# A diagonal complex recurrence over token chunks as rotated real scans, with its parameter tables moved one stage ahead

## Chip, core and metric

One core of a Trainium2 chip runs the whole kernel. The metric is the device time of one execution in microseconds (us), lower is better. PE is the matrix engine, PEld its weight loads, DVE the vector engine, ACT the scalar engine, POOL the general engine, SP the engine whose queue issues nearly all DMAs.

## The reference, cut to what matters

The program is one inference step of a two-layer network on 512 latent and 128 context tokens of 1024 channels. Each layer normalizes, projects, runs three mixers side by side (a Hyena long convolution, an S5 state space mixer, a gated DeltaNet), gates and projects their outputs, adds them up and projects again. The change concerns the S5 mixer: 64 groups of 16 channels, each with a diagonal state of 64 complex numbers, scanned forward and backward.

```python
for d in range(2):                               # forward, backward
    lam = lax.complex(lam_re[d], lam_im[d])
    step = jnp.exp(log_step[d])[:, None]
    lam_bar = jnp.exp(lam * step)                # parameters only
    b_bar = ((lam_bar - 1.0) / lam)[..., None] * lax.complex(b_re[d], b_im[d])
    seq = ug if d == 0 else jnp.flip(ug, axis=1)
    bu = jnp.einsum('gph,blgh->blgp', b_bar, seq.astype(jnp.complex64))
    bu = bu.at[:, 0].add(lam_bar * init)
    _, xs = lax.associative_scan(_lin_combine, (broadcast(lam_bar), bu), axis=1)
    finals.append(xs[:, -1])
    yd = einsum(c_re, xs.real) - einsum(c_im, xs.imag)
    y = y + (yd if d == 0 else jnp.flip(yd, axis=1))
```

`lam_bar` does not depend on the data: its powers, `b_bar` and the read-out factors are functions of the parameters alone.

## The kernel before, in words

The residual stream is kept transposed, channels on partitions and the 640 tokens along the free axis. Every projection (`load_w`, `mm3`, `proj`) splits weights and activations into a high and a low part and runs three float32r products; ACT writes the high part of the weights (L69), DVE or POOL the low part (L70), PE multiplies (L91). PE tile names tell who asks: `pj` is a projection of a mixer or of the merge, `pg` is one of 40 gate column tiles or the Hyena branch projection. The `pg` work depends only on the normalized input, so it can stand anywhere after it.

`start` loads the tokens, transposes them and computes the first modulation vectors. Then each layer has three stages. The first runs S5 and Hyena in turns, eight column tiles of 128 channels each: `run` takes one step of `s5_core`, then one of `hyena`, and so on, and emits 14 of the gate tiles behind them (L190). The second is the DeltaNet (`gdn`) with the other gate tiles. The third is `merge`: GLU of the S5 output, branch projections, output projection, residual, sums of squares for the next norm. `norm_h` stands at the head of a layer.

The code does not write out the order on an engine. A planner takes the instructions, walks a simulated time and gives each engine, whenever it is free there, the ready instruction that was emitted first. On the chip each engine, and each DMA queue, then keeps that order: an instruction that waits holds all that stands behind it on its engine. The layer-1 tables of the kernel before stand in the trace well ahead of their layer for that reason.

In S5, `s5_tables` (L685) makes the powers 0 to 8 of `lam_bar` (`PR`, `PI`), its powers over 8, 16, .. 128 tokens (`LR`, `LI`, `L2`) and the factor of `b_bar`, at the head of `s5_core`. The tokens lie in chunks of 8, 80 chunks in all (64 latent, 16 context). For each column tile:

- `s5_in` (L773) projects the input, sends it through DRAM (`us`) into the layout `U` (8 tokens x 16 channels on partitions, groups and chunks along the free axis), forms the increment matrices `M2` on DVE and POOL (L824 to L829), transposes them on PE, copies them out (L835), multiplies by `U` (L839, with 96 columns) and copies the state increments of the 80 chunks to `X`, laid out chunk, re/im, group (L841, ACT). Forward states lie on partitions 0 to 63, backward ones on 64 to 127.
- `s5_scan` (L845) runs the recurrence. Five segments of 16 chunks go side by side, and 16 steps follow one another. Each step is five DVE instructions on at most 80 elements, which write `Z` and `W` (`step`, L884 to L888), and two ACT copies that put the state before the step into `X` in place of the increment (L895). Then the states that enter the later segments are carried over (`C`) and their contributions added to `X` (`D`, `E`, L912 to L916). POOL makes the powers of the chunk step for that (`FR`, `FI`, L865 to L871).
- `s5_out` (L919) forms read-out matrices `M3` (L949 to L954), the kernels of the convolution inside a chunk (`K`, through DRAM `ks`, to `M1`), and sums three products per group: two of `M3` with `X`, whose columns lie 16 elements apart (L981, L982), and one of `M1` with `U` (L983).

`s5_in` and `s5_scan` of tile i + 1 are emitted ahead of `s5_out` of tile i. The S5 part has one PSUM bank (`pms`).

Of the kernel before, what the change touches and what calls it, by code (L numbers as in the profile page):

```python
# [20 lines left out]
NLAT = 512  # L21
# [17 lines left out]
# column tiles (128 wide) of the packed weights  # L39
# [13 lines left out]
def bc(ap, shape):  # L53
    return ap.to_broadcast(shape)


class Net:
# [4 lines left out]
    # ---------------------------------------------------------------- helpers  # L62
# [24 lines left out]
    def mm3(self, o, kh, wh, wl, xh, xl, s, m=128):  # L87
        """o += w^T x[:, s] over k tiles 4 kh .. 4 kh + 3"""
# [13 lines left out]
    def proj(self, l, t, xh, xl, q):  # L102
        """column tile t of x @ w: [128, 640] on two banks"""
# [8 lines left out]
    def conv(self, y, P, w, b, t=None):  # L112
        """3 taps along the tokens of each segment; t: space that moves a tap to ACT and Pool"""
# [26 lines left out]
    def wrap(self, pool, x, shape, phase, tag):  # L140
        """x (+ pi/2 if phase) folded into [-pi, pi]"""
# [13 lines left out]
    # ---------------------------------------------------------------- whole  # L155
# [75 lines left out]
    def start(self):  # L231
        """x^T with the grid embedding, sums of squares, first modulation vectors"""
        tc, nc, a = self.tc, self.nc, self.a
        self.xd = [self.dp.tile([KT, 128, NTOK], F32, name="xd%d" % i) for i in range(self.depth)]
# [17 lines left out]
        with self.pool(name="st", bufs=2) as p:  # L252
            xi = [p.tile([128, DM], F32, name="xi%d" % t, bufs=1) for t in range(5)]
            for t in range(5):
                nc.sync.dma_start(xi[t], a["x"][t * 128:(t + 1) * 128])
            pos = [p.tile([128, KT // 2, NLAT], F32, name="pos%d" % h, bufs=1) for h in range(2)]
            for h in range(2):
                nc.sync.dma_start(pos[h], a["pos"][4 * h:4 * h + 4].rearrange("k p t -> p k t"))
            wm = []
            for s in range(4):  # L260
                wm.append(p.tile([128, KT, 4, 128], F32, name="wm%d" % s, bufs=1))
# [1402 lines left out]
```

## Time and profile before

| | |
|---|---|
| time, median of 3 runs | 3792.77 us (3789.83 to 3797.14) |
| span of the profiled execution | 3792.6 us |
| PE busy | 3401.0 us (90%) |
| DVE busy | 2607.9 us (69%) |
| POOL busy | 1692.8 us (45%) |
| ACT busy | 1521.2 us (40%) |
| mean granted clock of PE | 0.941 |
| DMA | 362.89 MB, 96 GB/s, 16 engines 32% busy |

The stages of the profiled execution, in us from its start: start and first norm to 55, S5 and Hyena of layer 0 to about 1003, DeltaNet to about 1660 and merge, overlapping, to about 1940, norm to 1963, S5 and Hyena of layer 1 to about 2910, DeltaNet to about 3500, merge and final norm to the end.

[...]

### The profile page before, as it was taken

Reading aid. Unit: us, or ns where it says so; the run is one execution under the profiler, and the core shown is the slowest. Engines: PE = TensorE matmul, PEld = TensorE weight load, DVE = VectorE, ACT = ScalarE, POOL = GpSimd, SP = SyncE. Lnnn points to the kernel's source line nnn. Section 1 sums busy time; section 2 is a strip of 40 time slices with the busy share of each in tenths; the row PEclk is TensorE's granted clock in tenths of the full one; section 3 lists DMA queues with packets and bytes.
Section 4 is the critical chain, followed back from the end, with each engine's and each line's share of the span. In section 5 each row is a group of like instructions: output and inputs, shape, how many; then the busy total and the mean of one; then the engine's idle time right before and its main releaser. Section 6 shows DMA issues by size and latency. Waiting matters only on the chain. (4 is left out here: it accounts for less than half of the span.)

```text
span 3792.6 us, 70255 instructions
## 1 busy us (share of the span) xinstructions
PE 3401.0 (90%) x25850; PEld 3246.1 (86%) x25850; DVE 2607.9 (69%) x6113; ACT 1521.2 (40%) x3519; POOL 1692.8 (45%) x2083
## 2 busy tenths in 40 slices
PE   6898988888989898899978899899899898798998
PEld 5788977788989888899977889898889898798998
DVE  6988788889237874643749788878883278776354
ACT  4533333333244555443334333333332445555422
POOL 4656555555344444301226565666654454351010
PEclk8899999999989999899989999999999899899999
DMA  6322233432231212543632222222222312224352
GB/s 226 113 75 67 75 94 103 119 97 58 79 86 63 71 60 71 175 141 111 197 104 77 73 65 73 75 81 72 72 61 73 96 63 78 61 92 140 126 176 89
DMA packets 310615, 362.89 MB, mean 96 GB/s; under 512 B 86814, under 2 KB 190270, under 8 KB 310016
## 3 DMA queue, kind: packets, MB, share of 16 engines
q1 hardware_dynamic: 305368, 357.75, 31.0%
q8 instruction: 204, 3.34, 0.4%
q10 hardware_dynamic: 4904, 0.66, 0.1%
q14 instruction: 139, 1.14, 0.1%
HBM read 291.74 MB, written 66.54 MB: 94 GB/s over the span
## 5 line engine op out<-in xcount | busy, mean ns | idle before, releaser
L91 PE MATMUL pj<-hh,wh 128*128 128x320 f32 x2048 | 670.7, 328 | 77.5 <-ACT wh L69 32.4
L91 PE MATMUL pj<-hl,wh 128*128 128x320 f32 x2048 | 662.0, 323 | 2.4 <-DVE hl L70 2.4
L91 PE MATMUL pj<-hh,wl 128*128 128x320 f32 x2048 | 660.0, 324 | 2.8 <-POOL wl L70 1.5
L69 ACT CAST wh<-wr 128x512 fp32r<-128x512 f32 x608 | 375.0, 618 | 598.4 <-PE pj L91 396.9
L70 POOL TENSOR_TENSOR wl<-wr,wh 128x512 fp32r<-128x512 f32 x288 | 382.4, 1331 | 517.0 <-ACT wh L69 466.9
L91 PEld LDWEIGHTS pj<-hh,wh 128*128 128x128 f32 x2048 | 404.3, 197 | 89.7 <-ACT wh L69 33.7
L91 PE MATMUL pg<-hh,wh 128*128 128x320 f32 x1280 | 416.6, 326 | 14.1 <-ACT wh L69 10.2
L91 PE MATMUL pg<-hl,wh 128*128 128x320 f32 x1280 | 412.8, 323 | 0.0
L70 DVE TENSOR_TENSOR wl<-wr,wh 128x512 fp32r<-128x512 f32 x320 | 244.1, 764 | 244.5 <-ACT wh L69 242.1
L91 PE MATMUL pg<-hh,wl 128*128 128x320 f32 x1280 | 409.9, 324 | 1.6 <-POOL wl L70 1.6
L91 PEld LDWEIGHTS pj<-hl,wh 128*128 128x128 f32 x2048 | 403.2, 197 | 6.5 <-DVE hl L70 5.3
L91 PEld LDWEIGHTS pj<-hh,wl 128*128 128x128 f32 x2048 | 402.4, 197 | 5.9 <-POOL wl L70 2.8
L91 PE MATMUL pj<-yh,wh 128*128 128x320 f32 x1024 | 316.8, 311 | 3.6 <-ACT yh L69 2.4
L91 PE MATMUL pj<-yl,wh 128*128 128x320 f32 x1024 | 317.4, 311 | 2.4 <-DVE yl L70 2.3
L91 PE MATMUL pj<-yh,wl 128*128 128x320 f32 x1024 | 316.4, 310 | 0.0
L895 ACT COPY X<-Z 64x80 f32<-64x80 f32 x512 | 131.1, 256 | 386.7 <-DVE Z L888 380.1
L91 PEld LDWEIGHTS pg<-hh,wh 128*128 128x128 f32 x1280 | 252.1, 197 | 18.9 <-ACT wh L69 11.3
L91 PEld LDWEIGHTS pg<-hh,wl 128*128 128x128 f32 x1280 | 249.1, 196 | 4.1 <-POOL wl L70 2.7
L91 PEld LDWEIGHTS pg<-hl,wh 128*128 128x128 f32 x1280 | 251.7, 197 | 0.7 <-issue 0.4
L888 DVE TENSOR_TENSOR Z<-Z,X 64x80 f32<-64x80 f32 x512 | 209.0, 408 | 13.7 <-ACT X L841 1.1
L91 PEld LDWEIGHTS pj<-yh,wh 128*128 128x128 f32 x1024 | 192.5, 189 | 4.9 <-ACT yh L69 3.2
L91 PEld LDWEIGHTS pj<-yl,wh 128*128 128x128 f32 x1024 | 192.8, 188 | 4.2 <-DVE yl L70 4.2
(513 smaller groups left out, 8757.1 us busy)
## 6 DMA issues: line engine op xcount, KB each, us to landing
wr<-in_wt SPq DMA_DIRECT2D x608, 256.0 KB, 2.7
gt<-gst SPq DMA_DIRECT2D x160, 160.0 KB, 2.0
gt<-gt SPq DMA_DIRECT2D x64, 320.0 KB, 3.3
wr<-in_wmod SPq DMA_DIRECT2D x64, 256.0 KB, 3.1
Pm<-gcd SPq DMA_DIRECT2D x32, 320.0 KB, 11.2
wm<-in_wmod SPq DMA_DIRECT2D x4, 2048.0 KB, 18.6
M<-ks SPq DMA_DIRECT2D x256, 32.0 KB, 1.8
xd<-x SPq DMA_DIRECT2D x16, 320.0 KB, 4.3
```

Of the source, the lines that this page charges most:

```text
L69: self.nc.scalar.copy(h, src)
L70: (eng or self.nc.vector).tensor_tensor(l, src, h.bitcast(F32), op=ALU.subtract)
L91: ins = self.nc.tensor.matmul(o, w[:, k, :m], x[:, kh * 4 + k, s], start=kh == 0 and k == 0 and i == 0, stop=kh == 1 and k == 3 and i == 2)
L888: nc.vector.tensor_tensor(out[h], out[h], x, op=ALU.add)
L895: nc.scalar.copy(xv, S[h])
```

## The change

The complex factor over a chunk is split into its modulus and a turn. Increments are turned back by the power of the turn that belongs to their chunk, then the recurrence has a real factor and needs one real scan for the real part and one for the imaginary part, along all chunks of all eight groups at once; the result is turned forward again. The columns of a group are now 83: a slot for the initial state, 64 latent chunks, a slot, 16 context chunks, a slot. The factor array `A` holds the modulus in the chunk columns and 0 in the slots, where the state is reset.

- `s5_scan` is gone, with its 16 steps, the carries and the POOL powers. In `s5_in` the PSUM result is not copied by ACT; four DVE instructions per 3, 3 and 2 groups turn it into `X`. Then four scan instructions (re and im, forward partitions and backward partitions) write `Z`. A new `s5_turn` turns `Z` into the states with six DVE instructions of 664 elements.
- `X` is now re/im, group, chunk, so that a group's columns are contiguous for the read-out products.
- The turns `E` (2 x 8 x 83 per tile) and a block `F` (8 x 73: powers for `M2` and `M3`, initial states, modulus, `b_bar`) depend on parameters alone. `s5_tables` computes them and writes them to DRAM, 664 KB and 292 KB per column tile; `s5_in` loads both back. For layer 0 this is emitted in `start`, ahead of the loads of `x`, position table and modulation weights, with the turns doubled on DVE, two tiles at a time; for layer 1 in `merge` of layer 0, between the branch projections and the output projection, with the turns doubled on POOL, one tile at a time. `b_bar`, made per tile by POOL in `s5_in` before, and the powers that ACT copied per tile (`T2`, `T3`), are in `F` now.
- The small loads go out on SP (parameters) and ACT (`sbr`, `sbi`). In `merge` the gate tile `gt` has 3 buffers instead of 4.

The diff, cut to its core (comments that it deletes and unchanged parts left out):

```diff
@@ start
+            tab = self.s5_tables(0, nc.vector, 2)
+            next(tab)
             for t in range(5):
                 nc.sync.dma_start(xi[t], a["x"][t * 128:(t + 1) * 128])
+            next(tab)
             for h in range(2):
                 nc.sync.dma_start(pos[h], ...)
             for s in range(4):
                 nc.sync.dma_start(wm[s], ...)
+            for _ in tab:
+                pass
@@ s5_tables
+        with self.pool(name="s5k", bufs=1) as cp:
+            with self.pool(name="s5t", bufs=1) as p:
+                T = self.s5_factors(l, cp, p)
+            yield 0
+            with self.pool(name="s5u", bufs=1) as p:
+                for c0 in range(0, 8, n):
+                    self.s5_turns(l, c0, n, p, T, eng)
+        yield 1
@@ s5_turns (new), H = 8 n groups
+        E = p.tile([128, 2, H, 83], F32, name="tE", bufs=nc_)
+        eng.tensor_copy(E[:, :, :, 1], T["V"][:, :, gq])
+        e = 1
+        while e < 82:
+            n = min(e, 82 - e)
+            s, d = slice(1, 1 + n), slice(e + 1, e + 1 + n)
+            sh = [128, 2, H, n]
+            t = x[:, :, :, 0:n]
+            eng.tensor_tensor(t, E[:, :, :, s], bc(E[:, 1:2, :, e:e + 1], sh), op=ALU.mult)
+            eng.tensor_tensor(E[:, :, :, d], E[:, :, :, s], bc(E[:, 0:1, :, e:e + 1], sh), op=ALU.mult)
+            eng.tensor_tensor(E[:, 0, :, d], E[:, 0, :, d], t[:, 1], op=ALU.subtract)
+            eng.tensor_tensor(E[:, 1, :, d], E[:, 1, :, d], t[:, 0], op=ALU.add)
+            e *= 2
...
+            nc.sync.dma_start(te[c0 + c].rearrange(...), E[:, :, s])
+            nc.sync.dma_start(tf[c0 + c].rearrange(...), F[:, s])
@@ s5_core
         for i in range(8):
-            now = st
+            now = self.s5_turn(l, i, p)
             if i < 7:
                 self.s5_in(l, i + 1, p, T)
-                st = self.s5_scan(l, i + 1, p, T)
             self.s5_out(l, i, p, T, *now)
@@ s5_in
+        F = p.tile([128, H, 73], F32, name="F5", bufs=2)
+        nc.sync.dma_start(F, T["tf"][ct].rearrange("p (g c) -> p g c", g=H))
...
+        E = p.tile([128, 2, H, 83], F32, name="E5")
+        nc.sync.dma_start(E, T["te"][ct].rearrange("p (r g c) -> p r g c", r=2, g=H))
+        for x, n in ((slice(1, 65), 64), (slice(66, 82), 16)):
+            nc.scalar.copy(A[:, :, x], bc(F[:, :, 40:41], [128, H, n]))
...
-        for st in range(2):
+        for g1, k in ((0, 3), (3, 3), (6, 2)):
...
-                    nc.tensor.matmul(pi[:, g * 128:g * 128 + 96], mt[:, g, :], U[:, gi * 80:gi * 80 + 96], ...)
-                nc.scalar.copy(X[:, :, r, ls].rearrange("p j g -> p g j"), ...)
+                    nc.tensor.matmul(pi[:, r, g, :], mt[r][:, g, :], U[:, g1 + g, :], start=True, stop=True)
+            x = X[:, :, ls, 1:83]
+            nc.vector.tensor_tensor(x, pi, bc(E[:, 0:1, ls, 1:83], sh), op=ALU.mult)
+            nc.vector.tensor_tensor(w, pi, bc(E[:, 1:2, ls, 1:83], sh), op=ALU.mult)
+            nc.vector.tensor_tensor(x[:, 0], x[:, 0], w[:, 1], op=ALU.add)
+            nc.vector.tensor_tensor(x[:, 1], x[:, 1], w[:, 0], op=ALU.subtract)
...
+        for r in range(2):
+            z, b = [y[:, r].rearrange("p g c -> p (g c)") for y in (Z, X)]
+            nc.vector.tensor_tensor_scan(z[lo], A[lo], b[lo], 0.0, op0=ALU.mult, op1=ALU.add)
+            nc.vector.tensor_tensor_scan(z[hi, n - 3::-1], A[hi, n - 1:1:-1], b[hi, n - 1:1:-1], 0.0, ...)
@@ s5_turn (new)
+        for r in range(2):
+            nc.vector.tensor_tensor(X[:, r], Z[:, r], re, op=ALU.mult)
+            nc.vector.tensor_tensor(W, Z[:, 1 - r], im, op=ALU.mult)
+            nc.vector.tensor_tensor(X[:, r], X[:, r], W, op=ALU.add if r else ALU.subtract)
@@ s5_out
-                nc.tensor.matmul(o, M3[:, 0, g, 1:9, :], X[:, :, 0, gi], start=True, stop=False)
+                nc.tensor.matmul(o, M3[:, 0, g, 1:9, :], X[:, 0, gi, 0:82], start=True, stop=False)
@@ merge
+        if l + 1 < self.depth:
+            for _ in self.s5_tables(l + 1, nc.gpsimd, 1):
+                pass
```

## Rows read from the trace of the kernel before

**Rows 1.** Busy time of the engines, the page.
```profile
PE 3401.0 (90%) x25850; PEld 3246.1 (86%) x25850; DVE 2607.9 (69%) x6113; ACT 1521.2 (40%) x3519; POOL 1692.8 (45%) x2083
```
**Rows 2.** Stretches: length; busy PE, PEld, DVE, ACT, POOL; PE clock, DMA share, GB/s.
```profile
0.00:55.00 55.00, 25.21 (x315) 19.14 (x315) 22.73 (x74) 14.88 (x33) 7.38 (x7) 0.81 0.88 317
50.00:200.00 150.00, 124.47 (x764) 115.52 (x765) 135.77 (x312) 79.87 (x185) 112.16 (x130) 0.85 0.34 107
200.00:1000.00 800.00, 715.00 (x5603) 664.52 (x5602) 652.58 (x1547) 274.51 (x747) 450.75 (x626) 0.95 0.30 85
2000.00:2100.00 100.00, 79.54 (x556) 74.31 (x555) 95.85 (x225) 46.89 (x132) 61.26 (x86) 0.91 0.25 74
2100.00:2900.00 800.00, 737.94 (x5404) 706.68 (x5404) 634.99 (x1461) 281.43 (x752) 466.76 (x628) 0.95 0.26 72
900.00:1000.00 100.00, 94.01 (x697) 88.85 (x697) 61.28 (x126) 24.11 (x58) 46.92 (x50) 0.98 0.30 73
2800.00:2900.00 100.00, 93.45 (x690) 89.32 (x690) 66.49 (x143) 25.48 (x66) 49.01 (x54) 0.95 0.30 75
3000.00:3100.00 100.00, 95.69 (x807) 93.73 (x807) 67.14 (x148) 48.86 (x99) 56.02 (x59) 0.97 0.23 78
3200.00:3400.00 200.00, 175.86 (x1621) 167.53 (x1620) 147.65 (x412) 109.41 (x251) 95.97 (x110) 0.91 0.26 76
1600.00:1900.00 300.00, 296.99 (x2047) 295.25 (x2046) 152.83 (x306) 111.96 (x186) 48.22 (x19) 1.00 0.47 151
```
**Rows 3.** Waits of PE, 200 to 1003 us: us in total, times, longest.
```profile
PE pb L965 <- DVE T L936: 16.1, 5, 4.4
PE pg L286 <- DMA wr<-in_wmod: 11.6, 9, 2.1
PE pb L659 <- DVE KO L596: 6.1, 3, 3.7
```
**Rows 4.** Whole span, instructions on tile Z alone: busy PE, PEld, DVE, ACT.
```profile
0.00:3793.00 3793.00, 13.84 (x320) 11.54 (x320) 482.83 (x1392) 147.61 (x592) 0.94 0.32 96
```
**Rows 5.** The same for tile D: busy DVE.
```profile
0.00:3793.00 3793.00, 112.22 (x192) 0.94 0.32 96
```
**Rows 6.** Groups by line: shapes, count | busy us, mean ns | idle before.
```profile
L544 DVE TENSOR_TENSOR F<-pb,dec 128x512 f32<-128x512 f32 x64 | 43.6, 682 | 2.8 <-PE pb L531 2.4
...
L359 DVE TENSOR_TENSOR xn<-x,rs 128x640 f32<-128x640 f32 x16 | 13.2, 835 | 4.0 <-ACT hf L362 3.8
...
L950 DVE TENSOR_TENSOR m3t<-T,sci 128x640 f32<-128x640 f32 x32 | 41.7, 1304 | 0.2
...
L895 ACT COPY X<-Z 64x80 f32<-64x80 f32 x512 | 131.1, 256 | 386.7 <-DVE Z L888 380.1
...
L700 POOL TENSOR_TENSOR smag<-c,smag 128x64 f32<-128x64 f32 x2 | 21.1, 10546 | 0.7 <-DVE smag L698 0.7
```
**Rows 7.** Timeline of PE in one s5_out: start us, us, instruction.
```profile
314.57 0.46 PE L981 MATMUL pb<-X,M 128*128 128x80 f32 x2
314.85 0.45 PE L982 MATMUL pb<-X,M 128*128 128x80 f32 x2
315.13 0.36 PE L983 MATMUL pb<-U,M 128*128 128x80 f32 x2
315.33 0.46 PE L981 MATMUL pb<-X,M 128*128 128x80 f32 x2
```
**Rows 8.** Timeline at the end of the merge of layer 0.
```profile
1934.25 0.15 DVE L138 TENSOR_SCALAR rsv<-pb 128x5 f32<-128x5 f32 x1
...
1937.66 1.10 POOL L827 TENSOR_TENSOR M<-T,BI 128x512 f32<-128x512 f32 x1
...
1941.05 1.19 POOL L338 TENSOR_TENSOR rstd<-rsv,c 128x5 f32<-128x5 f32 x1
...
1945.75 0.31 POOL L865 TENSOR_TENSOR FR<-FR,LR 128x64 f32<-128x64 f32 x1
```
**Rows 9.** Timeline, the first projection of layer 0.
```profile
54.67 0.64 PE L91 MATMUL pj<-hh,wh 128*128 128x320 f32 x1 [8.57 <-ACT hh L69]
```

More of the change, by code (lines that the diff above doesn't have):

```diff
@@ L233, in start @@
         tc, nc, a = self.tc, self.nc, self.a
+        self.s5d = [[self.dp.tile([8, 128, n], F32, name="t%s%d" % (x, i)) for x, n in (("e", 1328), ("f", 584))]
+                    for i in range(self.depth)]
         self.xd = [self.dp.tile([KT, 128, NTOK], F32, name="xd%d" % i) for i in range(self.depth)]
@@ L819, in s5_in @@
+        A = A.rearrange("p g c -> p (g c)")
+        X = p.tile([128, 2, H, 83], F32, name="X5", bufs=2)
+        for g1, k in ((0, 3), (3, 3), (6, 2)):
+            ls = slice(g1, g1 + k)
+            M2 = p.tile([128, 2, 3, 128], F32, name="M2", tag="M23")[:, :, 0:k]
+            sh = [128, k, 8, 16]
             m2v = M2.rearrange("p r g (t h) -> p r g t h", t=8)
-            tv = [bc(x.rearrange("p t g -> p g t")[:, ls, :].unsqueeze(3), sh) for x in T2]
+            tv = [bc(F[:, ls, 8 * i:8 * i + 8].unsqueeze(3), sh) for i in range(2)]
@@ L829, in s5_in @@
             nc.gpsimd.tensor_tensor(m2v[:, 1], m2v[:, 1], tmq, op=ALU.add)
+            mt = []
             for r in range(2):
                 pt = self.bank()
-                for g in range(4):
+                for g in range(k):
                     self.tr(pt[:, g * 128:(g + 1) * 128], M2[:, r, g, :])
-                mt = p.tile([128, 4, 128], F32, name="mt", tag="mtm", bufs=2)
-                nc.scalar.copy(mt, pt.rearrange("p (g c) -> p g c", g=4))
-                pi = self.bank()
-                for g in range(4):
-                    gi = st * 4 + g
-                    nc.tensor.matmul(pi[:, g * 128:g * 128 + 96], mt[:, g, :], U[:, gi * 80:gi * 80 + 96],
-                                     start=True, stop=True)
@@ new lines, in s5_in, with s5_turn @@
+        self.s5x = Z, E, U, F
+    def s5_turn(self, l, ct, p):
+        nc, a = self.nc, self.a
+        H = 8
+        gq = slice(ct * H, ct * H + H)
+        lo, hi = slice(0, 64), slice(64, 128)
+        Z, E, U, F = self.s5x
+        re, im = E[:, 0], E[:, 1]
+        X = p.tile([128, 2, H, 83], F32, name="X5", bufs=2)
+        for r in range(2):
+            W = p.tile([128, H, 83], F32, name="W5")
+            nc.vector.tensor_tensor(X[:, r], Z[:, r], re, op=ALU.mult)
+            nc.vector.tensor_tensor(W, Z[:, 1 - r], im, op=ALU.mult)
+            nc.vector.tensor_tensor(X[:, r], X[:, r], W, op=ALU.add if r else ALU.subtract)
+        fs = p.tile([128, H, 2], F32, name="fs")
+        for h, s in ((lo, 81), (hi, 64)):
+            for r in range(2):
+                nc.scalar.mul(fs[h, :, r], X[h, r, :, s], -1.0 if r else 1.0)
+        for d in range(2):
+            nc.sync.dma_start(a["ns_out"][0, l, d, gq].rearrange("g p c -> p g c"), fs[64 * d:64 * d + 64])
+        return X, U, F
@@ L848, in s5_scan, with s5_out @@
+    def s5_out(self, l, ct, p, T, X, U, F):
         nc, a = self.nc, self.a
@@ L929, in s5_out @@
             nc.sync.dma_start(ld[n], a[n][l, :, g0 * 16:(g0 + H) * 16].rearrange("p (g h) -> p g h", g=H))
[L931 to L936 removed]
+        BR, BI = F[:, :, 41:57], F[:, :, 57:73]
         BZ, ks = T["BZ"], T["ks"]
@@ L944, in s5_out @@
             sh = [128, 4, 10, 16]
-            tv = [bc(x.rearrange("p t g -> p g t")[:, ls, :].unsqueeze(3), sh) for x in T3]
+            tv = [bc(F[:, ls, 16 + 10 * i:26 + 10 * i].unsqueeze(3), sh) for i in range(2)]
             cr, ci = [bc(x[:, ls, :].unsqueeze(2), sh) for x in (ld["scr"], ld["sci"])]
@@ L1417, in gate @@
     def gate(self, p, i):
[L1418 removed]
+        t = p.tile([128, NTOK], F32, name="gt", tag="gt", bufs=3)
         self.nc.sync.dma_start(t, self.gt[i])
```

283 lines of the change are left out of this document (137 added, 146 removed).

## The prediction

> **What bounds the kernel now.** First the busy times: PE 3401 of 3792.6 us, DVE 2608 [rows 1]. An average over the stages says little, so the second view is that of stretches. The merge keeps PE at 297 of 300 us with the full clock [rows 2]; nothing in DVE can be gained there. The S5 and Hyena stages, 948 us in each layer, are different. In 200 to 1000 us PE is busy 715 of 800 and DVE 653, in 2100 to 2900 PE 738 and DVE 635 [rows 2]. Two engines that wait for each other stand at 80 to 90% both. [...] Third the waits of PE in that stage: of the three longest in total two end at DVE (22 us) and one at a DMA (11.6), and none is over 4.4 us at a time [rows 3]. Gate tiles fill the long ones; PE loses by many small misses of an order fixed in advance. The gate tiles flow over the borders of the stages: what the first stage doesn't use, the DeltaNet has. So the time is PE's work plus PE's losses, summed over the whole span, and the change is to be read as work off PE, plus losses that a calmer DVE takes away, minus what the new tables cost at the seams. The profiled span, 3792.6, is the median of the runs (3792.77) to 0.01%, so the sum needs no correction.
>
> As measure of a stretch I take PE's busy share minus the missing clock (1 - clock): 0.894 - 0.05 = 0.844 in 200 to 1000, 0.922 - 0.05 = 0.872 in 2100 to 2900.
>
> **The change part by part.**
>
> *DVE, removed.* Everything on `Z` takes 482.8 us, everything on `D` 112.2 [rows 4, 5]; the two share no instruction. That is 595 us over 16 column tiles, 37.2 per tile. The carries on `C`, the products into `E` and some memsets come on top; I leave them out.
>
> *DVE, added.* The turn back from PSUM: a product of 512 elements from PSUM takes 0.682 [rows 6], so 492 elements 0.66; with a floor of 0.15 for the smallest instruction [rows 8] and 1.08 ns per element, the line through 0.15 and the 0.835 of 640 elements [rows 6], a sum of 246 elements takes 0.42, or 0.6 beside a busy POOL. Two groups of three: 2 x (2 x 0.66 + 2 x 0.55) = 4.8; one of two: 1.8; together 6.6. The turn forward: six instructions of 664 elements, between 0.86 (as in the norm, 0.835 for 640) and 1.35 (as in `s5_out`, 1.304 [rows 6]); I take 1.15, 6.9. The scans: no scan is in this trace. Four of 663 elements cost at least the 0.86 of a plain product each; above, I double the contended row, 2.6. I take 1.3, nearest to the row for instructions with two operands in this stage: 5.2. Three instructions more for `M2`, 0.6. Sum 19.3, bounds 16 to 26.
>
> *DVE, net.* 37.2 - 19.3 = 18 us per tile, 144 per layer, 287 in all; bounds 11 to 21 per tile. A tile takes about 110 us now, so an 800 us stretch holds 7.3 tiles and loses 131 us of DVE: 653 becomes 522.
>
> *What PE makes of it.* The trace has stretches where PE meets a DVE so loaded: 900 to 1000 (DVE 61%, PE 94.0, clock 0.98), 2800 to 2900 (66%, 93.5, 0.95), 3000 to 3100 (67%, 95.7, 0.97) [rows 2]. Their measure is 0.92, 0.885, 0.927, mean 0.911. At 0.91 the stretch 200 to 1000 shrinks by 800 x (1 - 0.844/0.91) = 58 us, 2100 to 2900 by 33, and DVE then stands at 522/742 = 70% in layer 0, the upper end of those rows. Sum -91. Bounds: 0, if the misses don't depend on DVE, and -124 at the 0.93 of the best of the three.
>
> *The heads of the two stages.* 50 to 200 measures 0.83 - 0.15 = 0.68, 2000 to 2100 0.795 - 0.09 = 0.705 [rows 2]. There DVE is at 90 and 96%, and no tile has yet come through its scan. Halfway to 0.91 gives -22 and -13; since part of the first is the norm itself, I take -25 (0 to -45).
>
> *PE's own work.* From start to start, a read-out product with `X`, columns 16 elements apart, takes 0.28, the one with `U`, contiguous, 0.20 [rows 7]. With `X` contiguous two products per group save 0.08 each: 2 x 0.08 x 128 groups (8 x 16) = 20.5, minus 1 for two columns more. The increment products fall from 96 columns to 82, up to 3. I take -22.
>
> *ACT.* The 512 copies into the slots (131 us [rows 6]) and the copies of the increments go; array `A`, slots and split copies come. ACT is 34% busy in 200 to 1000 [rows 2] and nobody waits long for it: 0.
>
> *Tables, layer 0.* Emitted first, they win DVE and POOL whenever ready. Two powers on POOL take 10.5 each [rows 6]. The doubling for two tiles is 28 instructions and 7776 elements: 28 x 0.15 + 7776 x 1.08 ns = 12.6, four times, 50 us of DVE; the factors are some 80 instructions, most of 64 elements, at 0.22 by the same line 18 us. DVE has 32 us free of the first 55 [rows 2], but of these a third passes before the first power is there. What is queued behind on DVE: adds of the position table, sums of squares, diagonal for the norm, the norm; behind these ACT's high parts and the first projection, at 54.67 [rows 9]. In exclusive order it would slip by the 50 + 18 - 22 = 46 us that don't fit; but part of that work stood after 54.67 before, on the same DVE (136 of 150 us in 50 to 200), and chains of dependent instructions leave gaps for others. I take +15, bounds -10 to +45. The DMA writes, 8 x 956 KB, come after the modulation weights; at 317 GB/s they are 25 us of engines that are 34% busy in 50 to 200 [rows 2].
>
> *Tables, layer 1.* On POOL a 64-element instruction takes 0.31, a 512-element one 1.10 [rows 8]: 0.20 plus 1.76 ns per element. One tile is 28 x 0.20 + 3888 x 1.76 ns = 12.4 and 6.6 for the 22 small ones of `F`; eight tiles 152, plus 21 for the powers, 173 us. POOL has 252 us free in 1600 to 1900 [rows 2]: hidden. Behind them on POOL stand the adds of the branches and the power for `rstd`. The latter waited before, too: `rsv` was there at 1934.4, the power began at 1941.05, behind `b_bar` and `M2` of layer 1 [rows 8]. If the tables are done by then, 5 us are won; if a table instruction is due each time, a few are lost. I take -5 (-6 to +20). The writes stand in SP's queue, in front of weight loads that have four buffers of 24 products each; a product takes 300 / 2047 = 0.147 there [rows 2], so the cover is 14 us: 0, and up to +30 if POOL is late.
>
> *Loads per tile.* 956 KB at 317 GB/s are 3 us, single-buffered for `E`; the previous turn frees it before the next projection ends: 0. PSUM keeps one bank, now held until two DVE products have read it: inside the bounds of the stage.
>
> *DeltaNet of layer 1.* In 3200 to 3400 PE is busy 176 of 200 at clock 0.91 [rows 2]. Gate tiles that the first stage no longer burns in its gaps are left for such stretches: -8 (0 to -15).
>
> Sum: -91 - 25 - 22 + 15 - 5 - 8 = -136; 3793 - 136 = 3657.
>
> **The rivals.**
>
> *A, DVE was the bound, and more comes free.* The same product costs 0.835 in the norm and 1.304 in `s5_out` [rows 6], with POOL 56% busy there. The change also takes `FR`, `FI` and `b_bar`, some 10 us per tile, off POOL, so what stays on DVE gets shorter. The measure rises to 0.93: -74 and -50, heads -45, PE -22, boundary -5, DeltaNet -15, front 0: 3582. For it: DVE lies behind 22 of the 34 us of the three longest waits [rows 3]. Against: 2800 to 2900 has no more DVE work and measures 0.885. [...]
>
> *B, the order is the bound.* PE's misses come from an order planned on other durations than the chip's, and stay with a calmer DVE. Then only PE's work (-22) and a quarter of the stage (-23) remain, plus the front: 3763. For it: the waits are short and many, and those for the modulation weights (11.6) don't change [rows 3].
>
> *C, slower: the seams become the bound.* SP keeps its order. If the planner takes the 10.5 us powers and the doubling on POOL for shorter than they are, each of the eight table writes in the merge waits at the head of SP for POOL, up to the 19 us of a tile plus 5 of the write, less 14 of cover: 10 each, 80 us of a PE that never waits there now; with the full 45 at the front and 20 at `rstd` +145. It turns the result from the point where the stages give back less than 120: with half the stage's gain, 3793 - 22 - 58 + 145 = 3858. For it: POOL's late power held `rstd` before [rows 8]. Against: 252 free us.
>
> *D, it doesn't unload DVE.* If a scan took 5.8 instead of 1.3, the 18 us per tile were gone: -22 + 15, 3786.
>
> **How the numbers follow.** Forecast 0.52, A 0.18, B 0.14, C 0.10, D 0.06. The forecast's own range is 3600 to 3715. Eight in ten: below 3550 and above 3790 I leave one in ten each, A's deeper half and C. About 0.2% (7.6 us) is what can be told from no change: faster 0.84, same 0.06, slower 0.10.
>
> **What would show it.** Right: DVE near 2350 in all, PE busy 94% in the middle of both stages, clock 0.96 and more, read-out products at 0.20, S5 tiles less than 100 us apart. Wrong: the first projection after 75 us; PE gaps in the merge before 1900 that end with a weight load; SP waiting for POOL `tE`; `rstd` behind table work; scans over 2.6 us; or DVE down and PE's share as before, which is B.

## The result and the profile after

The change takes the kernel from 3794.95 to 3749.1 us, ratio 0.9878 [0.9864, 0.9892]: 46 us faster, where the forecast was 136: a third of it. The time lies outside the forecast's own range (3600 to 3715) and inside the wider one that was given eight chances in ten (3550 to 3790). The changed kernel run again beside the experiments (control) gave 0.9891 [0.9877, 0.9906]. A kernel whose order on every engine and queue is the changed kernel's (f_first) gave 0.9920 [0.9901, 0.9939]. The two differ in the places of `u` and `F` in SBUF and ran on different chips; which of the two makes the 0.3% is open, and control came out where its expectation had put it if the place matters (0.9864 to 0.9892). I therefore draw nothing from differences under 0.4% (15 us) between runs of different chips; smaller ones count only where the stages bear them out.

The page of the changed kernel, its busy times and two rows of its DMA issues (size, median us to landing), against [rows 1]:

```profile
PE 3371.6 (90%) x25850; PEld 3220.7 (86%) x25850; DVE 2447.6 (65%) x4795; ACT 1367.1 (36%) x3017; POOL 1887.7 (50%) x2233
te<-tE SPq DMA_DIRECT2D x16, 664.0 KB, 3.8
E<-te SPq DMA_DIRECT2D x16, 664.0 KB, 10.6
```

DVE loses 160 us and not the 260 that "near 2350" meant; POOL gains 195. The view of stretches, the columns of [rows 2], of the changed kernel:

```profile
50.00:200.00 150.00, 95.53 (x579) 84.45 (x572) 129.57 (x202) 49.70 (x99) 90.66 (x121) 0.72 0.47 154
200.00:1000.00 800.00, 742.77 (x5902) 698.47 (x5901) 573.22 (x976) 224.70 (x566) 475.54 (x517) 0.95 0.37 100
1600.00:1900.00 300.00, 266.87 (x1704) 258.70 (x1703) 162.27 (x272) 107.79 (x202) 219.81 (x435) 0.93 0.49 161
2000.00:2100.00 100.00, 86.58 (x606) 82.36 (x608) 87.52 (x116) 34.58 (x87) 64.68 (x60) 0.93 0.34 85
2100.00:2800.00 700.00, 657.55 (x5036) 634.73 (x5032) 509.58 (x824) 201.20 (x501) 439.97 (x472) 0.97 0.31 84
```

Compare each with its row of [rows 2]. The middle of both stages is better (PE 743 of 800 and 658 of 700, the clock of layer 1 up). The head of the first stage is much worse: PE 95.5 of 150 at 0.72, where it was 124.5. The merge, which PE filled to 297 of 300 at the full clock, is at 267 and 0.93, with POOL at 220. The first 100 us behind the first projection, before and in the changed kernel, show the head without the later start:

```profile
55.00:155.00 100.00, 86.53 (x515) 79.85 (x514) 87.70 (x187) 57.24 (x120) 75.97 (x81) 0.88 0.39 126
74.00:174.00 100.00, 67.60 (x346) 60.52 (x347) 85.65 (x118) 32.89 (x69) 63.36 (x80) 0.70 0.50 167
```

The next table cuts the profiled executions at landmarks read from their timelines: first projection, last Hyena tile written, last DeltaNet head written, and the same again in layer 1. Gate work flows over the borders, up to some 25 us.

| us | front | S5+Hyena 0 | DeltaNet 0 | merge, norm | S5+Hyena 1 | DeltaNet 1 | rest |
|---|---|---|---|---|---|---|---|
| before | 54.7 | 947.8 | 657.8 | 291.1 | 958.8 | 598.5 | 283.9 |
| changed | 73.7 | 951.6 | 606.3 | 324.1 | 892.4 | 608.5 | 289.8 |
| control | 74.5 | 958.0 | 604.4 | 324.0 | 899.1 | 612.0 | 290.0 |
| no_tab1 | 74.4 | 960.0 | 608.8 | 292.3 | 910.9 | 615.1 | 289.8 |
| no_tab0 | 72.8 | 894.1 | 619.2 | 338.6 | 898.0 | 604.0 | 292.2 |
| no_tabs | 73.3 | 891.3 | 615.7 | 302.9 | 900.8 | 602.7 | 291.9 |
| no_tabs_gt4 | 73.6 | 897.5 | 615.8 | 291.2 | 917.8 | 617.7 | 288.4 |
| combo1 | 73.4 | 954.4 | 607.6 | 295.8 | 899.8 | 601.8 | 283.5 |
| no_scan | 74.1 | 919.0 | 614.8 | 324.1 | 892.2 | 612.3 | 288.8 |
| scan2 | 73.5 | 1019.1 | 591.8 | 329.3 | 961.8 | 600.2 | 294.3 |
| no_rec | 60.0 | 889.0 | 647.1 | 333.4 | 857.5 | 614.0 | 285.7 |
| f_first | 74.2 | 965.7 | 605.3 | 324.0 | 903.7 | 611.0 | 289.4 |
| no_dbl0 | 63.4 | 963.8 | 606.7 | 327.8 | 908.3 | 613.8 | 291.6 |
| after_gt4 | 73.8 | 961.7 | 609.0 | 315.2 | 898.1 | 604.4 | 283.3 |
| before_gt3 | 54.6 | 948.4 | 657.0 | 298.7 | 961.9 | 616.1 | 290.0 |

Before against changed: +19, +4, -51, +33, -66, +10, +6. The stages don't hold the same products, though. In layer 0 the first stage has 6382 products of PE before, 6554 in the changed kernel and 6386 in no_tab0 and no_tabs; the DeltaNet behind it 4808, 4669 and 4765. At the merge's 0.147 us a product, the changed kernel does 25 us more gate work in that stage. So layer 0's stage gave some 20 us and not nothing, and 20 of the DeltaNet's 51 are work done earlier. Layer 1's stage gave about what was forecast (52 products fewer, 8 of the 66 us), and the merge took 33.

### The profile page after: what moved, and what is told of

Read it like the earlier page. It is cut to its first block, busy times and chain, and to the rows that moved or that the text cites. A ratio compares the mean times of both kernels' runs of the same rounds, so it can differ in the third digit from the quotient of the medians.

```text
span 3746.5 us, 68717 instructions
## 1 busy us (share of the span) xinstructions
PE 3371.6 (90%) x25850; PEld 3220.7 (86%) x25850; DVE 2447.6 (65%) x4795; ACT 1367.1 (36%) x3017; POOL 1887.7 (50%) x2233
## 5 line engine op out<-in xcount | busy, mean ns | idle before, releaser
L91 PE MATMUL pj<-hh,wh 128*128 128x320 f32 x2048 | 659.9, 323 | 55.1 <-ACT wh L69 21.0
L91 PE MATMUL pj<-hh,wl 128*128 128x320 f32 x2048 | 652.1, 320 | 0.6 <-POOL wl L70 0.6
L70 POOL TENSOR_TENSOR wl<-wr,wh 128x512 fp32r<-128x512 f32 x288 | 394.9, 1375 | 450.5 <-ACT wh L69 394.5
L70 DVE TENSOR_TENSOR wl<-wr,wh 128x512 fp32r<-128x512 f32 x320 | 265.7, 832 | 234.0 <-ACT wh L69 231.1
L91 PE MATMUL pj<-yl,wh 128*128 128x320 f32 x1024 | 324.0, 317 | 8.5 <-DVE yl L70 8.2
L91 PEld LDWEIGHTS pj<-yh,wl 128*128 128x128 f32 x1024 | 197.2, 193 | 0.0
L675 POOL TENSOR_TENSOR Y<-p,p 128x256 f32<-128x256 f32 (+1 forms) x96 | 81.7, 852 | 173.1 <-DVE p L674 149.4
## 6 DMA issues: line engine op xcount, KB each, us to landing
E<-te SPq DMA_DIRECT2D x16, 664.0 KB, 10.6
```

The source lines that it names most:

```text
L70: (eng or self.nc.vector).tensor_tensor(l, src, h.bitcast(F32), op=ALU.subtract)
L91: ins = self.nc.tensor.matmul(o, w[:, k, :m], x[:, kh * 4 + k, s], start=kh == 0 and k == 0 and i == 0, stop=kh == 1 and k == 3 and i == 2)
L675: nc.gpsimd.tensor_tensor(Y[:, fs, 0, :], p1[:, :nf, 0, :], p2[:, :nf, 0, :], op=ALU.subtract)
```

## The experiments

Three theories. S: the seams took back what the stages gave (tables at the front, tables and one gate buffer less in the merge). M: the stages gave less than forecast. B: PE's misses belong to the planned order. Ratios are to the kernel before, run on the same chip; 0.01 is 38 us.

**Leaving the tables out.** no_tab1:

```diff
-        if l + 1 < self.depth:
-            for _ in self.s5_tables(l + 1, nc.gpsimd, 1): pass
-        te, tf = self.s5d[l]
+        te, tf = self.s5d[0]
```

> Leaves out the tables of layer 1 in the merge, their powers, doublings and writes; layer 1 reads the tables of layer 0, so its numbers change and its work doesn't. Theory S (the seams took back what the stages gave): the merge regains the 40 us that it lost against the kernel before (its gate and projection part 241 us against 212, the output projection 66 against 57); time 3703 to 3718. Theory M (the stages gave less than forecast, the seams cost only the 19 us of the later first projection): within 10 us of the changed kernel, 3739 to 3750.

Measured 0.9875 [0.9858, 0.9893]. The merge came back by 32 us against the control, as S said, and the total hardly moved, as M said: layer 1, whose code is the same, took 15 us more. no_tab0:

```diff
-            tab = self.s5_tables(0, nc.vector, 2)
...
+            zt = p.tile([128, 1328], F32, name="zt0", bufs=1)
+            nc.gpsimd.memset(zt, 0.0)
+            for c in range(8):
+                nc.sync.dma_start(self.s5d[0][0][c], zt)
+                nc.sync.dma_start(self.s5d[0][1][c], zt[:, 0:584])
```

> Leaves out the computation of layer 0's tables at the front; the same DRAM rows are written from one zeroed tile, so writes and loads stay and the states of layer 0 are zero. Theory S: the 19 us of the later first projection come back and another 25 to 35 us at the head of the first S5 stage, where DVE works on tables until 137 us; time 3695 to 3710. Theory M: the first projection is back near 55 us and no more comes of it, 3728 to 3735.

Measured 0.9783 [0.9764, 0.9802], 41 us under the control. The first projection was still at 72.8, for a reason of the experiment's own. Two stretches and a wait of PE (us in total, times, longest) in no_tab0:

```profile
40.00:60.00 20.00, 5.78 (x69) 4.13 (x69) 2.13 (x12) 0.27 (x1) 0.00 (x0) 0.59 1.03 403
60.00:80.00 20.00, 3.50 (x10) 2.37 (x10) 11.41 (x15) 9.88 (x19) 7.80 (x8) 0.50 0.97 353
PE pj L91 <- ACT wh L69: 24.5, 1, 24.5
```

DMA stands at 1.03 and 403 GB/s while DVE idles: the zeroed rows, written at once, are in front of the loads that follow. The first weights are issued at 63.4, and ACT, which makes `wh`, waits 23.3 us for another load (`alt`). The gain is all in the S5 stage, 64 us shorter than the control's; 25 of them are gate work that stands later (DeltaNet and merge are 15 us longer each), so that some 40 remain, the gain of the total. That is between the two outcomes. no_tabs is both edits:

> Leaves out both: no table is computed, layer 0 reads zeroed rows and layer 1 the same ones. What is left is rotation, scans and the contiguous states. Theory S: the two savings add, 80 to 95 us under the changed kernel, 3655 to 3670, which is the recorded forecast without its 15 us for the front. Theory M: 3715 to 3735.

Measured 0.9706 [0.968, 0.9731], 70 us under the control (65 under the changed kernel's own ratio), again between the outcomes: the tables cost some 70 us, not the 10 of the forecast (front 15, boundary -5, merge 0). The writes of layer 0's rows and all loads are still in this run.

no_dbl0 keeps all but the doublings at the front:

```diff
-        e = 1
+        e = 1 if l else 82
+        if l == 0: g.memset(E, 0.0)
```

> Leaves out the doublings of layer 0's rotations, 116 instructions less on DVE at the front, 63 us of it; the rows are written at the same place with zeros, so layer 0's states are wrong and its work is as before. If DVE's table work delays the first tiles: first projection at 60 to 66 us, first S5 tile's inputs written before 95 us (112 in the changed kernel), 35 to 60 us faster, 3690 to 3715. If the head is slow for the table writes or for the missing gate work: within 15 us, 3735 to 3757.

Measured 0.9922 [0.9899, 0.9945]: no gain, a miss for S in the total. The front and the head did what S said: first projection 63.4, first S5 inputs written at 97 in place of 112, second tile's output at 392 where the control has it at 432 (with 93 products fewer by then, 14 of the 40 us). The middle lost it: from there to the eighth tile's output it took 590 us for the control's 558 (12 of the 32 for 80 products more), and the stages end at 1027 and 1032 with the same 6555 products. PE's order in layer 0 is not the control's, so the run doesn't say what the doublings alone cost; zeroing `E` also put memsets on POOL.

**The order.** no_dbl0's edit touches layer 0's tables alone. The programs show what the planner made of it: of some 10000 entries of PE in layer 1, about 2900 lines of difference against the changed kernel's order. no_tab1 has the same order there as no_dbl0, lazy_b and no_tabs_gt4 differ from it by under 100 and 300 lines; all other kernels with the changed kernel's layer 1 code differ from the changed kernel by some 400 lines or less. So layer 1 has two orders. The whole S5 stage of layer 1 in no_tabs and in no_tabs_gt4, columns as above:

```profile
1884.00:2784.00 900.00, 832.51 (x6216) 801.53 (x6217) 641.55 (x1010) 269.55 (x649) 534.07 (x562) 0.96 0.31 84
1878.00:2796.00 918.00, 848.14 (x6281) 814.01 (x6282) 635.38 (x1011) 273.74 (x657) 541.70 (x565) 0.96 0.32 84
```

DVE has 6 us less to do in the second and the stage is 18 us longer, with 65 more products in it (65 x 0.147 = 10 us). Stage and DeltaNet together are 1504 against 1536, and 1526 (no_tab1) against 1511 (control): an order that nobody asked for is worth up to 32 us, as much as most edits here. (One and the same order took 1501, 1511 and 1515 us in the changed kernel, the control and f_first, so the order's share is known to some 10 to 30 us.)

**Gate buffers.** before_gt3 is the kernel before with `bufs=3` in place of 4 for `gt`:

> The kernel before with one edit of the change alone: three buffers for the merge gates in place of four. My forecast took it at nothing. If gate buffers are part of what the merge lost: 5 to 20 us slower than before, in both merges, 3798 to 3815. If not: within 6 us of before.

Measured 1.0063 [1.0047, 1.0079], 24 us slower, more than either outcome. Of the difference between the traces 8 us are in the merge of layer 0 and 6 behind the DeltaNet of layer 1, as the expectation had it for the merges; 18 are in the DeltaNet of layer 1, where gate buffers are at most filled ahead. There the order is another too: counted as above, PE's order in layer 1 differs from the kernel before's by some 3400 lines. So 6 to 8 us per merge can be put down to the buffer, and the rest may be the order's. after_gt4 gives the changed kernel its fourth buffer back:

```diff
+        y = x[:, :, :, 0:16] if l else p.tile([128, 2, H, 16], F32, name="ty")
+            ld[n] = E[:, i, :, 67:83] if l else p.tile([128, H, 16], F32, name=n)
-        t = p.tile([128, NTOK], F32, name="gt", tag="gt", bufs=3)
+        t = p.tile([128, NTOK], F32, name="gt", tag="gt", bufs=4)
```

> The changed kernel with four buffers for the merge gates again, their room made by sharing the small temporaries of layer 1's tables; nothing is left out. The kernel before lost 24 us when it had three. If the smaller gate buffer is part of the time that the change gave back: 15 to 25 us faster than the changed kernel, 3724 to 3734 (and both merges some 8 us shorter). If late table work on POOL holds the gates whatever their number: within 6 us, 3743 to 3755.

Measured 0.9853 [0.9835, 0.9871], 14 us under the control and 25 under f_first, which ran beside it. Its two merges are 9 and 7 us shorter than the control's, as expected. And without any tables (no_tabs with `bufs=4`):

> As the run without any tables (both layers' tables left out, layer 0's rows zeroed, layer 1 reading the same), with four gate buffers as in the kernel before. It is the change without its seams. If the forecast's terms for the stages were right and the seams took the rest: 138 + 8 us under the kernel before, 0.959 to 0.965, that is 20 us or more under the run without tables (0.9706). If the stages gave less than forecast and the gate buffer costs nothing once the tables are gone: 0.969 to 0.972.

Measured 0.9726 [0.9709, 0.9742], just above the second outcome. Its merge is 12 us shorter than that of no_tabs, with the same products; layer 1, in the other order, took 32 us more, so the total can't tell the outcomes apart.

**What the merge pays with.** Waits of SP's queue in the merge of the control, then DVE's groups there (busy us, mean ns of one; the last takes one input from PSUM), then the same groups in no_tabs:

```profile
SPq L862 <- POOL tE L843: 41.2, 8, 9.2
SPq L1484 <- POOL m L1544: 23.1, 5, 6.9
```

```profile
L70 DVE TENSOR_TENSOR wl<-wr,wh 128x512 fp32r<-128x512 f32 x73 | 62.7, 862 | 81.5 <-ACT wh L69 81.3
L1496 DVE TENSOR_TENSOR yk<-yk,gt 128x640 f32<-128x640 f32 x8 | 11.1, 1390 | 8.7 <-DMA gt<-gt 8.7
L132 DVE SCALAR_TENSOR_TENSOR ga<-ga,gv 128x640 f32<-128x640 f32 x7 | 8.7, 1238 | 11.2 <-ACT gv L1527 11.1
L132 DVE SCALAR_TENSOR_TENSOR gt<-gt,pj 128x640 f32<-128x640 f32 x16 | 13.1, 816 | 14.3 <-PE pj L91 6.3 <-POOL tF L813 3.4 <-POOL tE L833 2.7
```

```profile
L70 DVE TENSOR_TENSOR wl<-wr,wh 128x512 fp32r<-128x512 f32 x76 | 53.6, 707 | 82.1 <-ACT wh L69 82.1
L1496 DVE TENSOR_TENSOR yk<-yk,gt 128x640 f32<-128x640 f32 x8 | 7.9, 993 | 5.6 <-DMA gt<-gt 4.1 <-DMA yk<-yd 1.5
L132 DVE SCALAR_TENSOR_TENSOR ga<-ga,gv 128x640 f32<-128x640 f32 x8 | 6.6, 826 | 6.2 <-ACT gv L1527 6.2
L132 DVE SCALAR_TENSOR_TENSOR gt<-gt,pj 128x640 f32<-128x640 f32 x16 | 13.1, 820 | 31.4 <-PE pj L91 29.1 <-DMA wr<-in_wt 2.3
```

All eight table writes held SP's queue, 41 us; the gate loads waited 23 us for sums that POOL did late; and beside the table work the three groups of DVE shown here with two inputs from SBUF took 1.2 to 1.5 times as long, while the one with an input from PSUM kept its time (816 for 820 ns). In te_pool the writes leave from POOL's queue (`(nc.gpsimd if l else nc.sync).dma_start(te...`, the same for `tf`):

> The 16 table writes of layer 1 are issued from POOL's queue, where they follow their producer, in place of SP's, where they held the queue for 40 us in the merge. Nothing is left out. If SP's order is how the merge pays: 20 to 40 us faster, 3710 to 3730. If POOL's load itself pays (slower DVE instructions beside it, gate buffers held by late POOL sums): within 6 us of the changed kernel, 3743 to 3755.

Measured 0.9922 [0.9901, 0.9942], slower than both outcomes, with a merge 10 us longer than the control's. SP no longer waits for `tE`, and nothing is won: SP's order alone is not how the merge pays. What the writes cost on POOL's queue was not measured. In tab1_dve layer 1's doublings run on DVE (`self.s5_tables(l + 1, nc.vector, 1)`):

> The doublings of layer 1's tables run on DVE in place of POOL, in the same place of the merge; nothing is left out. POOL loses some 170 of its 255 us of table work, DVE, 162 of 300 us busy there, gets about 67. If POOL's load pays the merge (DVE instructions made longer beside it, sums and table writes late): the merge of layer 0 comes back to within 12 us of the kernel before, and the time is 15 to 30 us lower, 3720 to 3735. If any table work in the merge costs the same: within 8 us, 3741 to 3757.

Measured 0.9859 [0.9845, 0.9874], 12 us under the control, too little to tell by itself. Its merge is 8 us shorter than the control's and still 25 longer than before: nearer to the second outcome. f_first emits the tile and load of `F` ahead of the projection:

```diff
+        F = p.tile([128, H, 73], F32, name="F5", bufs=2)
+        nc.sync.dma_start(F, T["tf"][ct].rearrange("p (g c) -> p g c", g=H))
         Pu = self.proj(l, W_S5 + ct, self.hh, self.hl, T["q"])
```

> The load of a column tile's factor table (F) is emitted ahead of its projection, in place of behind the write of u, which waits for the projection at the head of SP's queue; nothing is left out, and PE's order doesn't change. In the trace of the changed kernel DVE is idle for 64 us in all until these loads land, twelve times. If the chain of an S5 tile sets the pace, as doubling the scans suggests (112 us of DVE gave 115 us of time): 25 to 55 us faster, 3695 to 3725. If gate tiles or Hyena's work hide those waits: within 8 us, 3741 to 3757.

Measured 0.9920 [0.9901, 0.9939]: the planner had issued that load as early as its buffer allowed, no queue's order changed, and but for the places in SBUF the run is one more of the changed kernel. What an earlier `F` is worth it doesn't say. combo1 joins after_gt4, tab1_dve and f_first:

> Nothing is left out: four gate buffers, the factor load ahead of the projection and layer 1's doublings on DVE together. If the three add: 20 + 35 + 7, 3680 to 3700. If they are one and the same slack: 3715 to 3735.

Measured 0.9804 [0.9784, 0.9825], the best kernel that computes everything: 33 us under the control, 44 under f_first beside it and 75 under the kernel before, the outcome of "one and the same slack". The merge, its output projection included, in control and in combo1:

```profile
1637.00:1944.00 307.00, 276.99 (x1776) 270.56 (x1775) 155.42 (x243) 100.80 (x169) 224.60 (x448) 0.93 0.51 166
1635.00:1914.00 279.00, 267.55 (x1779) 265.08 (x1779) 189.12 (x474) 102.02 (x171) 111.94 (x215) 0.98 0.58 181
```

POOL from 225 to 112, DVE from 155 to 189, the clock from 0.93 to 0.98, 28 of the merge's 33 us back. Alone the buffer gave 9 of them and the doublings on DVE 8: together they give more than the two, so I take buffers and POOL's load for one wait with two ends.

**The front, emitted later.** lazy_a emits the tables of tiles 2 to 7 behind the norm, lazy_b also runs their doublings on POOL, combo2 is lazy_a with after_gt4 and tab1_dve:

```diff
                     self.norm_h(l)
+                if l == 0:
+                    for _ in self.tab: pass
```

> Nothing is left out: the changed kernel with layer 0's tables of tiles 2 to 7 emitted behind the norm, on DVE. Against the control: 10 to 30 us faster if the norm and the first tiles then come earlier; within 10 us if DVE's table work costs the same wherever it stands before tile 2.

> Nothing is left out. Layer 0's factors and the tables of its first two column tiles stay on DVE at the front; those of tiles 2 to 7 are emitted behind the norm and their doublings run on POOL. If DVE's table work at the front is what delays the norm and the first S5 tiles (the changed kernel has doublings on DVE until 136 us): first projection at 62 to 68 us, first S5 tile's inputs written before 100 us in place of 112, and 25 to 45 us faster, 3705 to 3725. If it is the 8 MB of table writes that come among the first weights (as the run without layer 0's tables suggests, where they held the first weights for 24 us), or POOL now becomes late: within 10 us, 3740 to 3760.

> Nothing is left out: four gate buffers and layer 1's doublings on DVE, as in combo1 (0.9804), and layer 0's tables of tiles 2 to 7 emitted behind the norm, still on DVE. If the front can be paid later: first projection before 70 us and 10 to 30 us under combo1, 0.973 to 0.978. If tables of layer 0 cost the same wherever DVE does them: 0.979 to 0.982.

Measured 0.9873 [0.9858, 0.9887], 1.0066 [1.0043, 1.0089] and 0.9820 [0.9802, 0.9838]. lazy_a and combo2 came out at the second outcome, lazy_b above both. Emission alone moves little: lazy_a's first projection is at 76.8. Nor are the runs clean: in lazy_a and combo2 the first `u` also waited, some 15 us, for POOL's table work whose place it takes. lazy_b lost to the place of its buffers, as the waits of ACT and PE between 60 and 200 us show:

```profile
ACT u L903 <- POOL tE L845: 45.6, 1, 45.6
PE pj L91 <- ACT u L904: 56.8, 1, 56.8
```

The first `u` of the stage lies where POOL's tables still were.

**What a microsecond of DVE is worth.** scan2 runs each scan twice (`for _ in range(2):` around the two calls):

> The changed kernel with each of the four scans of a column tile run twice, 64 scans more of 1.74 us by the trace of the changed kernel: 112 us of DVE, 56 in each S5 stage; nothing is left out. If the stages are worth what my forecast said (58 us of PE for 131 us of DVE in layer 0, 33 for 115 in layer 1): 56 x 0.44 + 56 x 0.29 = 41 us slower, 3780 to 3800. If the order bounds the stages and DVE's load does not (rival B): within 12 us, 3740 to 3761. If the chain of a tile (turn, scan, turn) sets the pace: 7 us a tile, up to 112, over 3830.

Measured 1.0181 [1.0164, 1.0198], 110 us over the control for 112 us of DVE, as if the chain of a tile set the pace. no_scan leaves out the scans and the products of `s5_turn`:

> The changed kernel without its scans and its turn forward, 64 scans of 1.74 us and 96 products and sums of 0.99 us, 206 us of DVE in all; the read-out takes the states as turned back. If DVE's time in a tile counts one to one in both directions, as the doubled scans had it: 0.94 or less. If less DVE is worth what the kernel before without its recurrence showed (113 us for 595, 0.19 each): 39 us under the changed kernel, 0.976 to 0.982. If the order alone bounds: 0.986 to 0.992.

Measured 0.9805 [0.979, 0.9821], 33 us for 206, the second outcome: the chain doesn't count one to one the other way. no_rec, on the kernel before:

```diff
-        for s in range(16):
-            ...
-        for m in range(3):
-            ...
```

> The kernel before without its recurrence: the 16 steps per column tile, the states' copies, the carries and the products D are left out, 595 us of DVE and 131 of ACT; the states that are read out are the bare increments. It shows what can be had from the stages at most. By the forecast's measure (PE share less missing clock of 0.93 at best): 74 + 50 in the middle, up to 45 at the heads, 130 to 170 us under the kernel before. If DVE's time in the chain of a tile counts one to one until PE's own work is the bound, as the doubled scans suggest (713 and 768 us of work in two stages of 948 and 959): 280 to 400 us. If the order bounds: under 80.

Measured 0.9708 [0.969, 0.9726], 113 us for 595 of DVE (and 131 of ACT), between the first outcome and the last. The middles of the two stages, in control, no_scan and no_rec:

```profile
200.00:1000.00 800.00, 734.33 (x5856) 690.72 (x5855) 567.18 (x973) 224.63 (x566) 475.62 (x511) 0.95 0.37 99
2100.00:2800.00 700.00, 654.38 (x4976) 631.77 (x4975) 508.08 (x818) 199.77 (x495) 437.72 (x467) 0.97 0.32 83
```

```profile
200.00:950.00 750.00, 694.20 (x5542) 653.70 (x5542) 466.14 (x872) 205.53 (x526) 413.67 (x474) 0.95 0.36 98
2100.00:2800.00 700.00, 658.82 (x5002) 637.53 (x5001) 426.44 (x750) 199.90 (x497) 395.60 (x444) 0.96 0.31 84
```

```profile
200.00:900.00 700.00, 674.76 (x5485) 630.91 (x5484) 425.57 (x815) 217.68 (x512) 451.82 (x595) 0.98 0.33 96
2100.00:2700.00 600.00, 596.07 (x4645) 579.92 (x4644) 362.85 (x652) 201.13 (x460) 381.87 (x431) 1.00 0.29 82
```

By the prediction's measure (PE share less missing clock): control 0.868 and 0.905, no_scan 0.876 and 0.901, no_rec 0.944 and 0.993. no_scan takes DVE from 71 and 73 to 62 and 61% and the measure stays; no_rec, with DVE at 61%, about as much as no_scan, has PE full in layer 1. So the measure isn't a function of DVE's load. That the order which the planner finds for other work decides is the likeliest reading and is not shown: no_rec also has no table work, less on ACT, longer read-out products, and copies the increments by ACT where the change holds the one PSUM bank for two DVE products. No run tests the last. In these three runs, each with its own order, a microsecond of added DVE work cost 1.0 and one of removed work gave 0.16 to 0.19.

## Why the prediction was wrong

**The front, +15.** Measured +19: right, from its bounds. What the step left out is what came behind. It counted the 50 us of doublings (62 in the trace) against the first projection alone.

**The heads, -25.** The step that failed first. Layer 1's was right: [rows 2] has 2000 to 2100 at 0.705, after it is 0.866 - 0.07 = 0.796, 9 us. Layer 0's went the other way: 50 to 200 fell from 0.68 to 0.637 - 0.28 = 0.357, which is 48 us of PE, 29 beyond the front's 19, where the step had forecast a gain. Table work is on DVE until 136 us, in front of the first S5 tiles; `u` of the first tile is written at 112 (75 before) and the second tile's output at 424 (349 before). The prediction took the work behind 54.67 as room for the tables and in the same breath counted the head as calmer; the sum used that time twice. That the tables' computation is what costs there is shown by no_tab0 (some 40 us); how much of it is the doublings is not.

**The middle, -91.** By the same measure 200 to 1000 went to 0.928 - 0.05 = 0.878 and 2100 to 2800 to 0.939 - 0.03 = 0.909: 800 x (1 - 0.844/0.878) = 31 and 800 x (1 - 0.872/0.909) = 33 us. By the measure layer 1 came out as forecast, layer 0 at half. The mechanism was read from three stretches in which DVE's load and PE's share went together; no_scan and no_rec show that one doesn't set the other, so layer 1's agreement is luck as far as the mechanism goes. Rival B, given 0.14, left a quarter of the gain, 23 us, to the two stages besides PE's own work. The runs put more there: without its tables layer 0's stage is 56 us shorter than before with the same products (no_tabs), and layer 1's, counted by its products, 58 in the changed kernel. That is 114 of the 138 us that the forecast gave to middle, heads and PE's work together. So layer 0's stage fell short mainly by the tables at its head.

**DVE's prices.** From the trace of the changed kernel:

```profile
L960 DVE TENSOR_TENSOR_SCAN Z<-A,X 64x664 f32<-64x664 f32 x32 | 56.2, 1758 | 4.9 <-ACT X L954 4.6
L961 DVE TENSOR_TENSOR_SCAN Z<-A,X 64x662 f32<-64x662 f32 x32 | 55.4, 1730 | 0.4
L977 DVE TENSOR_TENSOR X<-Z,E 128x664 f32<-128x664 f32 x32 | 30.4, 950 | 0.1
L978 DVE TENSOR_TENSOR W<-Z,E 128x664 f32<-128x664 f32 x32 | 32.3, 1010 | 0.2
L979 DVE TENSOR_TENSOR X<-X,W 128x664 f32<-128x664 f32 x32 | 32.0, 1001 | 0.3
```

The scan took 1.74 us where I took 1.3, 7.0 per tile for 5.2; the turn forward 0.99 for 1.15, 5.9 per tile for 6.9. The two nearly cancel. DVE ended above 2350 for the tables and because the 320 weight splits went from 764 to 832 ns, 22 us, beside a busier POOL (1888 us in all for 1693).

**PE's own work, -22.** A step over-sized by two. Read-out products at the full clock in the changed kernel (start, us), against [rows 7]:

```profile
2348.53 0.39 PE L1043 MATMUL pb<-X,M 128*128 128x82 f32 x2
2348.75 0.39 PE L1044 MATMUL pb<-X,M 128*128 128x82 f32 x2
2348.98 0.39 PE L1045 MATMUL pb<-U,M 128*128 128x82 f32 x2
2349.20 0.39 PE L1043 MATMUL pb<-X,M 128*128 128x82 f32 x2
```

Start to start `X` takes 0.22, not 0.20, and `U`, with 82 columns for 80, 0.22 where it was 0.20: 0.67 per group for 0.76, 128 x 0.09 = 12 us. The increment products, forecast at up to 3 us, went from 69.0 to 67.6 us busy.

**Tables of layer 1: hidden, 0.** Failed: +33 in merge and norm; without the tables 32 come back (no_tab1). The step compared POOL's need (173 us) with POOL's free time (252) and stopped there. POOL's busy time in the merge is 17 us without the tables (no_tabs) and 225 with them, so they took 208, and free time on POOL didn't hide them. What the rows show beside them is DVE's longer instructions, gate loads that waited for POOL's late sums with one buffer less, and a clock of 0.93; combo1 gets 28 us back by the buffer and the doublings on DVE. The SP wait that the prediction named is there (41 us), and te_pool, which has it no more, is no faster. That is rival C's place, with another mechanism than C's. The edit from four buffers to three was not costed at all; it is 4 to 12 us per merge (before_gt3, after_gt4, no_tabs_gt4).

**Boundary, -5.** Right: the power for `rstd` follows `rsv` at once, norm from 23.0 to 17.1 us. **Loads per tile, 0.** Right for `E`, though its load took 10.6 us and not 3; open for `F`, whose load stands behind the write of `u`. Waits of DVE over the whole span of the changed kernel:

```profile
DVE X L949 <- DMA E<-te: 0.4, 1, 0.4
DVE m2t L929 <- DMA F<-tf: 63.8, 12, 9.4
```

f_first was to show what the 63.8 us cost and left the load where it was.

**DeltaNet, -8.** Layer 1's is 10 us longer, layer 0's 51 shorter, of which 20 are gate work done elsewhere. The other 31 are luck: I didn't foresee them and no run tests them; no_rec, with less DVE work still, keeps 647 there.

**The sum.** Counted with 0.147 us for each product that moved, layer 0's first stage gave 21 us where middle, head and PE's work had some 85; the merge took 33 where 5 were to be won; the front took 4 more than forecast; layer 1's DeltaNet and the rest took 10 where 8 were to be won. Against that, layer 1's first stage gave 58 for some 53, and layer 0's DeltaNet the unforeseen 31, without which the change would have given some 15 us. Without tables the change is worth 112 us (no_tabs), where the forecast's terms for stages, PE and DeltaNet say 146: 34 short, although no_tabs has the better of layer 1's two orders and the DeltaNet's luck as well. The tables then cost 65 to 70 us instead of 10. That is S for two thirds of the missing 90 us, M and B for the rest. How the rest divides between M and B stays open, since nearly every edit also drew a new order.

## What to carry to other kernels

Work that moves to a seam need not be hidden by free time on its engine (POOL had 252 us free here, the tables took 208, and merge and norm became 33 us longer): count whose instructions get longer beside it, what shares its queue and its buffers, and what the new tiles push out (one gate buffer was 4 to 12 us per merge). A stretch's PE share tells what an order makes of a load, not what a lighter load would make of a new order; leave the suspected work out once before trusting a slope. And where a planner orders the program, an edit in one layer can redraw another: look there before crediting or blaming it. Compare stages by the work that they hold, too: 172 products had moved from one stage to another here.

## What the runs showed of the hardware

In the changed kernel a scan of 64 x 664 took 1.74 us, 1.76 times the product of 128 x 664 beside it (0.99). In the merge of the control, where POOL was 73% busy, three groups of DVE instructions with two SBUF inputs took 1.2 to 1.5 times as long as in no_tabs, where POOL had 17 us of work (862 for 707 ns, 1390 for 993, 1238 for 826), a fourth (`yl` from `yk` and `yh`) 1.07 times (1064 for 995), and one with an input from PSUM as long as there (816 for 820). What makes them longer was not measured. At a granted clock of 1.00 an fp32 read-out product with 82 contiguous columns took 0.22 us from start to start; with 80 columns, 16 elements apart, it had taken 0.28. SP's queue kept its order in the merge of the changed kernel: a weight load left at 1697.09, right behind the split that freed its buffer (ended 1697.06); the next such split ended at 1702.35, and the load left at 1705.46, behind a write of `tE` that had waited for POOL and left at 1703.60.
